# A decoder block on one core: attention halves stored apart and added by a loading DMA, first norms squared token by token, ten weight blocks kept in split form

## The chip, the core and the metric

The kernel runs on one core of one Trainium2 chip. The metric is device time in microseconds (us): the median of three runs of the kernel before is 1899.0 us (1898.85, 1899.0 and 1906.92). One further execution was taken by the hardware profiler; it took 1905.2 us, and its trace spans 1903.5 us. All durations and waits below come from that one execution.

The engines are named as in the profile: PE is TensorE (PEld its weight loads), DVE is VectorE, ACT is ScalarE, POOL is GpSimd, and SP is the queue that issues nearly all DMAs. Each engine, and the SP queue, works strictly in the order of its own instructions, and each instruction waits for the semaphores of what it needs.

## What is computed

One layer over 2048 tokens of width 1024, in float32:

```python
hn = rmsnorm(h, norm1_g)
proj = jnp.einsum('bsd,de->bse', hn, w_in)          # 1024 -> 2048: pool | q | k | v, 512 each
y_pool = pool_mixer(u_pool, pool_w, pool_scale)     # causal means over 2, 4, 8, 16 tokens
o = stick_breaking_attention(to_heads(q), to_heads(k), to_heads(v))   # 8 heads of 64
mixed = jnp.concatenate([rmsnorm(y_pool, pool_out_g), rmsnorm(y_attn, attn_out_g)], axis=-1)
h = h + jnp.einsum('bse,ed->bsd', mixed, w_out)
hn2 = rmsnorm(h, norm2_g)
act = jnp.square(jax.nn.relu(jnp.einsum('bsd,df->bsf', hn2, w_up)))
h = h + jnp.einsum('bsf,fd->bsd', act, w_down)
return rmsnorm(h, final_g)
```

## The kernel before

**Tiles.** The tokens are cut into NT = 4 tiles j of 512. Activations are held transposed: 128 features on the partitions, 512 tokens along the row. Every float32 operand of a product is *split* into a high and a low part in TensorE's own format (`split`, lines 142 to 146: ACT copies the high part at L145, DVE subtracts it at L146), and a product is three matmuls, high by high, high by low and low by high (L177 to L179).

**Input projection.** `w_in` is 16 blocks c of 1024 x 128; blocks 0 to 3 give the pool branch, 4 to 7 q, 8 to 11 k, 12 to 15 v. A block is loaded as one float32 tile `raw` of 512 KB (`load_raw`, two buffers) and split in two halves, *granules*, into tiles `hl` (`weights`, five buffers, WAHEAD = 5). A granule `hl` holds both parts and is again 512 KB. A product over one block is 24 matmuls into a PSUM tile `pd`, which has two buffers. `front(q)` treats the token tiles in pairs, (0, 1) and (2, 3). Six blocks (6, 10, 14, 7, 11, 15) are used for both tiles of a pair while they lie split in `hl`. The other ten, `EARLY` and `POOL`, are loaded and split anew for each of the four token tiles.

**First norm.** For tile 0 the squares are taken at once (`norm1_first`). For tiles 1 to 3 `norm1_rms` queues eight pieces of work: ACT squares a 128 x 512 chunk of the transposed x, DVE adds it to a sum `ss`. Then `mean_squares` sums over the partitions with matmuls by a column of 1/n (L204, PSUM tile `pm`), and `inv_root` computes the inverse root on POOL in small steps. `spread` (L230, tile `pr`) broadcasts it over the partitions with PE.

**Attention.** Weights of nearby keys alone are computed in the main path (`near`); a branch at the end handles the rest if any weight is left, and it isn't taken here. A unit is one head and two blocks of 128 queries: logits `pz` (L616, L617), two sigmoids on ACT (`sh`, `sg`), a mask on POOL (L647), a running product and a product on DVE, transposes `pta` (L663), a split into `at`, and products with v into `po` (L675). `po` holds the sum of the two parts in two halves of 64 partitions. `halves_sum` copies one half to SBUF on ACT (L633) and adds the other on DVE (L634), into a tile `ot` (one buffer) that two heads share; when both are in, one DMA of 256 KB stores it to `os_` in DRAM (L682). `attn_norm` later loads `os_` in two DMAs of 512 KB (L796, into `yb` for tiles 0 and 1, into `ol` for 2 and 3) and takes squares of what it loaded.

**What sets the order.** The Python code queues work in a list (`prog`) of products and notes, with small pieces (`later`) and attention units (`todo`) put between them by paces. Then a scheduler that models the times places every engine's instructions, the DMA issues among them. So the order on each engine is fixed before the run, and with a change in one place it moves everywhere in this first part. The first part (input projection, attention, output projection) fills the trace to about 690 us. After it come the up and down projections (PSUM tiles `pX`, `pY`, `pZ`, `pb`), done by a scheme with seven products in place of eight, which the change doesn't touch.

The DRAM tiles `hs` are read at the end by POOL's accumulating DMAs (L1249, `add_residual`), which load from DRAM and add to what stands in SBUF. They are the only ones of that kind before the change.

Of the kernel before, what the change touches and what calls it, by code (L numbers as in the profile page):

```python
# [15 lines left out]
P = 128  # L16
# [28 lines left out]
@with_exitstack  # L45
def hymba_block(ctx: ExitStack, tc: tile.TileContext, xT, gains, w_in, pool_w, w_out, w_up, w_down, out):
    nc = tc.nc
# [81 lines left out]
    vs = [[dram.tile([P, T], F32R, name=f"vs{h}_{j}") for j in range(NT)] for h in range(H)]  # L129
    os_ = [dram.tile([H // 2, P, T], F32, name=f"os{j}") for j in range(NT)]  # L130
# [25 lines left out]
    def load_raw(i):  # L156
        while len(raws) <= min(i, len(wlist) - 1):
            raw = wp.tile([P, 2, G, P], F32, tag="raw", name="raw")
            last_load[0] = nc.sync.dma_start(raw, wlist[len(raws)].rearrange("p (x k) c -> p x k c", x=2))
# [47 lines left out]

    def inv_root(pm, eng):
# [3 lines left out]
        nc.vector.tensor_scalar(m, pm, 1.0, EPS, op0=ALU.mult, op1=ALU.add)  # L212
        eng.tensor_scalar(y.bitcast(I32), m.bitcast(I32), -0.5, float(0x5F3759DF), op0=ALU.mult, op1=ALU.add)
# [19 lines left out]

    def inv_rms(ss, n, r=None, eng=None, early=False):

        eng = eng or nc.gpsimd
        with tc.high_priority():
            y = inv_root(mean_squares([ss], n, psz if early else None, "pz" if early else "px"), eng)
            yr = tmp.tile([P, 2, TB], F32R, tag="yr", name="yr")
            eng.tensor_copy(yr[:, 0], y)  # L240
            eng.tensor_tensor(yr[:, 1], y, yr[:, 0].bitcast(F32), ALU.subtract)
            where, tag = (psx, "px") if eng is nc.vector else (psz, "pz") if early else (pst, "pt")
            pr = where.tile([P, T], F32, tag=tag, name="pr")
            marks["pr"] = spread(pr, yr)
            if eng is not nc.vector:
                g = state["tick"]
                gates.extend([(g + 10, marks["pm"]), (g + 14, marks["pr"])])
# [38 lines left out]

    wlist = []
    prog = []

# [17 lines left out]
    def start():  # L307
# [4 lines left out]
        def weight(c, x):  # L312
            nc.sync.dma_start(raws[c][:, x], wlist[c][:, x * G:(x + 1) * G])

# [32 lines left out]

    def norm1_rms(j):
        def square(k):
            if k == 0:  # L350
                st[j]["ss"] = sum_tile()
            add_square(st[j]["ss"], st[j]["x"][:, k], k == 0)
        later.extend(lambda k=k: square(k) for k in range(KD))
        later.append(lambda: st[j].update(r=inv_rms(st[j]["ss"], D, root_tile() if j == 2 else None, early=j == 1)))

# [92 lines left out]
    def in_proj(j, c, again=False):  # L448
        if not again:
            wlist.append(w_in[c])  # L450
        if c < 4:
# [103 lines left out]
    def tail(first):  # L555
# [24 lines left out]
        for j in range(NT):  # L580
# [3 lines left out]
            for c in range(KD):  # L584
# [10 lines left out]
                if c == 3 and j == NT - 1:  # L595
                    note(begin_ffn)
                wlist.append(w_out[c])
                step(2, lambda w, j=j, c=c: dense(j, "m", w, lambda ps: add_acc(j, c, ps)))
# [37 lines left out]
    def near_unit(j, h, p, t):  # L636
# [40 lines left out]
        if p == 1:  # L677
            if h % 2 == 0:
                t["ot"] = ots[j, h // 2] = att.tile([P, T], F32, tag="ot", name="ot", bufs=1)
# [5 lines left out]
    ots, stages = {}, []  # L685

# [51 lines left out]
    def far(j):  # L738
        first = 2 if j == 0 else 0
        for h in range(H):  # L740
# [38 lines left out]
            on = att.tile([P, T], F32, tag="sh", name="onear")  # L779
            nc.sync.dma_start(on[me, f0:], os_[j][h // 2][me, f0:])  # L780
            nc.vector.tensor_tensor(ot[me, f0:], ot[me, f0:], on[me, f0:], ALU.add)
            nc.sync.dma_start(os_[j][h // 2][me, f0:], ot[me, f0:])


    def attn_norm(j, make=None):
        part = {}

        def load():
# [854 lines left out]
```

## Time and profile before

| | |
|---|---|
| median of three runs | 1899.0 us |
| the profiled execution: time / span of its trace | 1905.2 / 1903.5 us |
| DVE busy | 1480.9 us (78%) |
| ACT busy | 1023.7 us (54%) |
| POOL busy | 242.1 us (13%) |
| DMA packets | 535.91 MB, mean 282 GB/s |

A row of the page's groups reads: line, engine, operation, out<-in and shapes, number, then busy time and the mean of one in ns, then how long the engine stood idle just before them and what ended that. A row of waits reads: who waited, for whom, total us, times, longest. A row of the table by stages reads: the stage, its length, busy us of each engine with the number of instructions, the granted clock of TensorE, the share of the DMA engines' time, and GB/s.

Work beside PE in the first part is spread over DVE, ACT and the DMA queue as follows:

```profile
50.00:100.00 50.00, 49.30 (x242) 41.07 (x241) 43.60 (x79) 27.41 (x48) 16.43 (x35) 1.00 0.65 212
```

Here DVE is busy for 43.60 of 50 us, ACT for 27.41, and PE for 49.30.

### The profile page before, as it was taken

How to read it: one execution, taken by the hardware profiler on the slowest of the kernel's cores; microseconds unless marked ns; L12 is line 12 of the kernel's file. 1: busy time of each engine (PE TensorE's matmuls, PEld its weight loads, DVE VectorE, ACT ScalarE, POOL GpSimd, SP SyncE). 2: the span in 40 equal slices, each digit the busy share in tenths (PEclk: the TensorE clock that was granted, in tenths of full speed). 3: DMA queues.
4: the chain of work that ended last, by engine and by line, in shares of the span. 5: the costliest groups of instructions: out<-in, count | busy, mean ns of one | idle time of the engine just before them, and what ended most of it. 6: DMA issues, size and time to landing. Idle time of an engine off the chain costs nothing.

```text
span 1903.5 us, 26682 instructions
## 1 busy us (share of the span) xinstructions
PE 1869.5 (98%) x8883; PEld 1555.5 (82%) x8883; DVE 1480.9 (78%) x2151; ACT 1023.7 (54%) x1616; POOL 242.1 (13%) x463
## 2 busy tenths in 40 slices
PE   9999999999999999999999999999999999999997
PEld 7888788888888888778888888887788888888886
DVE  6887799668866976778699988786566677888774
ACT  5565466555544465554557555554332665656543
POOL 0333233223421050000000000000010010020120
PEclk9999999999999999999999999999999999999998
DMA  6686696798788867887899888889999899999752
GB/s 224 204 269 196 191 308 213 239 322 278 272 316 306 296 229 254 284 306 276 286 365 334 313 300 278 301 284 326 378 311 326 289 322 301 334 297 342 290 210 91
DMA packets 222164, 535.91 MB, mean 282 GB/s; under 512 B 26048, under 2 KB 32192, under 8 KB 218176
## 3 DMA queue, kind: packets, MB, share of 16 engines
q1 hardware_dynamic: 217264, 525.46, 79.2%
q0 software_dynamic: 4608, 8.39, 2.4%
q8 instruction: 72, 1.18, 0.3%
q14 instruction: 76, 0.62, 0.1%
q10 hardware_dynamic: 144, 0.26, 0.0%
HBM read 349.46 MB, written 184.55 MB: 281 GB/s over the span
## 4 chain that ended last, share of the span: by engine, by line
PE 45%; DMA 6%; DVE 4%; issue 2%; ACT 1%; POOL 0%; SPq 0%; DVEq 0%; ACTq 0%
PE pb L1274 14%; PE pb L1451 12%; PE pY L1101 10%; PE pZ L1101 5%; PE pX L1101 2%; DMA ar<-sd 1%; DVE hw L146 1%; DMA ar<-sdi 1%; PE pb L1391 1%; DMA t<-in_w_down_dram 1%; DMA su<-hs 0%; DMA sd<-a 0%; DMA td<-t 0%; DMA sdi<-a 0%; DMA b<-in_w_down_dram 0%
## 5 line engine op out<-in xcount | busy, mean ns | idle before, releaser
L1101 PE MATMUL pY<-sa,hw 128*128 128x512 f32 x1536 | 366.3, 389 | 3.0 <-ACT u L1024 2.6
L1101 PEld LDWEIGHTS pY<-sa,hw 128*128 128x128 f32 x1536 | 288.0, 188 | 64.3 <-ACT u L1024 3.9
L1274 PE MATMUL pb<-ad,wd 128*128 128x512 f32 x1344 | 305.1, 389 | 0.3 <-DVE ad L146 0.3
L177 PE MATMUL pd<-h,hl 128*128 128x512 f32 x752 | 299.0, 398 | 3.5 <-DVE acc L813 2.0
L179 PE MATMUL pd<-h,hl 128*128 128x512 f32 x752 | 297.6, 396 | 0.0
L178 PE MATMUL pd<-h,hl 128*128 128x512 f32 x752 | 297.5, 396 | 0.0
L1274 PEld LDWEIGHTS pb<-ad,wd 128*128 128x128 f32 x1344 | 252.2, 188 | 53.1 <-DVE ad L146 0.7
L1451 PE MATMUL pb<-ad,wd 128*128 128x512 f32 x1104 | 253.9, 390 | 2.4 <-ACT ad L145 2.0
L1451 PEld LDWEIGHTS pb<-ad,wd 128*128 128x128 f32 x1104 | 206.5, 188 | 46.1 <-ACT ad L145 2.4
L146 DVE TENSOR_TENSOR ad<-ar,ad 128x1024 fp32r<-128x1024 f32 x160 | 193.9, 1220 | 44.6 <-ACT ad L145 44.2
L145 ACT ACTIVATE ad<-ar 128x1024 fp32r<-128x1024 f32 x160 | 168.2, 1053 | 95.2 <-PE pb L1451 32.0
L1101 PE MATMUL pZ<-sa,hw 128*128 128x512 f32 x768 | 187.0, 390 | 1.1 <-DVE a L1044 1.0
L1101 PEld LDWEIGHTS pZ<-sa,hw 128*128 128x128 f32 x768 | 143.7, 188 | 32.4 <-DVE a L1044 2.6
L177 PEld LDWEIGHTS pd<-h,hl 128*128 128x128 f32 x752 | 142.6, 190 | 31.8 <-issue 2.8
L145 ACT ACTIVATE hl<-raw 128x512 fp32r<-128x512 f32 x168 | 104.2, 631 | 116.2 <-PE pd L179 66.1
L179 PEld LDWEIGHTS pd<-h,hl 128*128 128x128 f32 x752 | 142.5, 189 | 28.2
L178 PEld LDWEIGHTS pd<-h,hl 128*128 128x128 f32 x752 | 142.5, 190 | 26.8
L146 DVE TENSOR_TENSOR hl<-raw,hl 128x512 fp32r<-128x512 f32 x168 | 113.9, 684 | 45.8 <-ACT hl L145 45.5
L1018 ACT ACTIVATE a<-a 128x512 f32<-128x512 f32 x96 | 60.1, 629 | 97.4 <-DVE a L1060 43.0
L146 DVE TENSOR_TENSOR hw<-rt,hw 128x512 fp32r<-128x512 f32 x128 | 86.3, 683 | 26.0 <-ACT hw L145 26.0
L145 ACT ACTIVATE wd<-wq 128x1024 fp32r<-128x1024 f32 x56 | 59.3, 1060 | 76.8 <-PE pb L1274 68.1
L146 DVE TENSOR_TENSOR wd<-wq,wd 128x1024 fp32r<-128x1024 f32 x56 | 68.4, 1221 | 34.2 <-ACT wd L145 34.2
(218 smaller groups left out, 2736.2 us busy)
## 6 DMA issues: line engine op xcount, KB each, us to landing
ar<-sd SPq DMA_DIRECT2D x96, 512.0 KB, 5.7
ar<-sdi SPq DMA_DIRECT2D x64, 512.0 KB, 5.8
rb<-in_w_up_dram SPq DMA_DIRECT2D x30, 1024.0 KB, 6.6
sd<-a SPq DMA_DIRECT2D x104, 256.0 KB, 5.1
raw<-in_w_in_dram SPq DMA_DIRECT2D x50, 512.0 KB, 4.8
sdi<-hr SPq DMA_DIRECT2D x96, 256.0 KB, 5.5
wr<-in_w_down_dram SPq DMA_DIRECT2D x48, 512.0 KB, 5.6
sd<-s SPq DMA_DIRECT2D x88, 256.0 KB, 4.7
```

The lines of the kernel that those rows point to most:

```text
L145: nc.scalar.activation(hi, src, AF.Copy)
L146: return nc.vector.tensor_tensor(lo, src, hi.bitcast(F32), ALU.subtract)
L177: nc.tensor.matmul(ps, hl[:, 0, c], hi, start=(k == 0), stop=False)
L178: nc.tensor.matmul(ps, hl[:, 0, c], lo, start=False, stop=False)
L179: mm = nc.tensor.matmul(ps, hl[:, 1, c], hi, start=False, stop=(k == n - 1))
L1018: nc.scalar.activation(t, src, AF.Relu)
L1101: nc.tensor.matmul(t, w[:, wx, c], a[:, ax, c % 2], start=first and c == 0 and x == 0, stop=last and c == G - 1 and x == 2, skip_group_che ...
L1274: nc.tensor.matmul(b, t[:, wx, 2 * (kk % 2) + c, i * P:(i + 1) * P], a[:, ax, c], start=p in ("P1", "P5", "P2") and kk == 0 and c == 0 and ...
L1391: nc.tensor.matmul(b[:, cols], block(t, wx, c, n), a[:, ax, c, cols], start=False, stop=(i == 1 and c == 1 and x == 2), skip_group_check=True)
L1451: nc.tensor.matmul(ps[q, n], block(t, wx, c, n), left_[q][:, ax, c], start=(n_ in ("P1", "P3") and kk == 0 and c == 0 and x == 0), stop=(n ...
```

## The change

Three edits.

1. **Ten blocks kept split.** The first time that a block of `EARLY + POOL` is split, each `hl` is also stored to a DRAM tile `ws` (20 stores of 512 KB). The three later uses load `hl` straight from there, 512 KB for each granule, in place of a 512 KB load for two granules and two splits. So 60 of 168 splits go from ACT and from DVE, 30 loads of `raw` go, and 60 loads of `hl` come.
2. **First norms by tokens.** For tiles 1 to 3 a second copy of x with tokens on the partitions is loaded in eight tiles `xrow` of 256 KB. ACT squares each with its accumulator output, which leaves the sum of each token's 512 squares in one column of `ss`. POOL adds two columns for each token. The seven adds of DVE and the matmuls of `mean_squares` go for these three norms.
3. **Halves stored apart.** ACT copies the whole of `po` (128 x 512) to `ot`, and two DMAs of 128 KB for each head store its halves to `os_[j][0]` and `os_[j][1]`; the add on DVE goes. `attn_norm` loads the first halves with SP as before and then adds the second ones with two accumulating DMAs of 512 KB that POOL issues. A wait is added by that: POOL's DMA waits for the SP load into the same tile.

```diff
+    ws = {c: [dram.tile([P, 2, G, P], F32R, name=f"ws{c}_{x}") for x in range(2)] for c in EARLY + POOL}
...
     def load_raw(i):
         while len(raws) <= min(i, len(wlist) - 1):
+            if wlist[len(raws)][1] == "split":
+                raws.append(None)
+                continue
...
-            last_split[0] = split((hl[:, 0], hl[:, 1]), raws[i // 2][:, i % 2])
+            use, kept = wlist[i // 2][1:]
+            if use == "split":
+                nc.sync.dma_start(hl.bitcast(F32), kept[i % 2].bitcast(F32))
+            else:
+                last_split[0] = split((hl[:, 0], hl[:, 1]), raws[i // 2][:, i % 2])
             grans.append(hl)
             load_raw(i // 2 + 1)
+            if use == "keep":
+                nc.sync.dma_start(kept[i % 2].bitcast(F32), hl.bitcast(F32))
...
     def norm1_rms(j):
+        def load(k):
+            nonlocal rows
+            rows = ntp.tile([P, T], F32, tag="nt", name="xrow")
+            nc.sync.dma_start(rows, x[j, k // 2, :, k % 2])
...
-            add_square(st[j]["ss"], st[j]["x"][:, k], k == 0)
+                parts = sum_tile()
+            nc.scalar.activation(rows, rows, AF.Square, accum_out=parts[:, k:k + 1])
+            if k + 1 < KD:
+                load(k + 1)
+        def total():
+            two = parts[:, 0:KD].rearrange("p (b i) -> p b i", i=2)
+            nc.gpsimd.tensor_tensor(parts[:, KD:KD + TB], two[:, :, 0], two[:, :, 1], ALU.add)
...
-            halves_sum(ots[j, h // 2], po, h % 2)
-            if h % 2:
-                nc.sync.dma_start(os_[j][h // 2], ots.pop((j, h // 2)))
+            ot = att.tile([P, T], F32, tag="ot", name="ot", bufs=1)
+            nc.scalar.activation(ot, po, AF.Copy)
+            me = slice(h % 2 * DH, (h % 2 + 1) * DH)
+            for x in range(2):
+                nc.sync.dma_start(os_[j][x, h // 2, me], ot[x * DH:(x + 1) * DH])
...
-                nc.sync.dma_start(ol[i], os_[j][2 * i:2 * i + 2].rearrange("c p t -> p c t"))
+                nc.sync.dma_start(ol[i], os_[j][0, 2 * i:2 * i + 2].rearrange("c p t -> p c t"))
+            for i in range(2):
+                nc.gpsimd.dma_start(ol[i], os_[j][1, 2 * i:2 * i + 2].rearrange("c p t -> p c t"), accum_op=ALU.add)
```

How it moves instructions, at three places. The line numbers are each kernel's own; in the changed one L146 and L147 split, L173 loads a kept granule, L679 is the mask and L828 and L830 are the two loads of the attention's halves.

**ACT, up to the attention norm of tile 0** (second pair of tiles, near 360 us in the trace): the rows from the second `mix` tile, whose store stands just ahead of SP's load of `yb`, to the first square `ss` of that load. Before:

```order
343 L145 ACTIVATE mix<-nt 128x512
344 L437 ACTIVATE vf<-pd 128x512
345 L145 ACTIVATE mix<-nt 128x512
346 L145 ACTIVATE hl<-raw 128x512
347 L145 ACTIVATE vt<-ptv 128x8x64
348 L145 ACTIVATE mix<-nt 128x512
349 L437 ACTIVATE vf<-pd 128x512
350 L145 ACTIVATE hl<-raw 128x512
351 L184 ACTIVATE ss<-yb 128x512
```

And in the changed kernel, where the second `mix` stands in row 302:

```order
306 L146 ACTIVATE mix<-nt 128x512
307 L467 ACTIVATE vf<-pd 128x512
308 L146 ACTIVATE hl<-raw 128x512
309 L146 ACTIVATE vt<-ptv 128x8x64
310 L146 ACTIVATE at<-pta 128x512
311 L654 ACTIVATE sh<-pz 128x512
312 L656 ACTIVATE sg<-pz 128x512
313 L146 ACTIVATE qk<-pd 128x512
314 L654 ACTIVATE sh<-pz 128x512
315 L656 ACTIVATE sg<-pz 128x512
316 L146 ACTIVATE hl<-raw 128x512
317 L194 ACTIVATE ss<-yb 128x512
```

Seven rows stand between the second `mix` and the square before, and fourteen in the changed kernel (303 to 316): the first square of the loaded halves has moved back by seven instructions.

**POOL, at the same norm**: in the changed kernel the two accumulating loads stand between an inverse root and the masks of the next attention units; before there was nothing there.

```order
188 L253 CAST yr<-v 128x4
189 L254 TENSOR_TENSOR yr<-v,yr 128x4
190 L830 DMA yb<-os_244 128x2x512 x2
191 L679 AFFINE_SELECT sg<-sg 128x2x128
192 L691 COPY left_139<-pc 128x2
193 L679 AFFINE_SELECT sg<-sg 128x2x128
```

Whatever these loads wait for, the masks behind them now wait for too.

**SP, at the attention norm of tile 1** (near 410 us): `h<-mx` loads operands of the output projection, `mx` is where the normed branches are stored, `vs` holds v. Before:

```order
336 L547 DMA h<-mx_4_252 128x1024
337 L547 DMA h<-mx_5_253 128x1024
338 L547 DMA h<-mx_6_254 128x1024
339 L796 DMA yb<-os_245 128x2x512 x2
340 L609 DMA qa<-qs_2_174 128x512
341 L701 DMA vw<-vs_2_234 128x128
342 L703 DMA vw<-vs_3_235 128x512
343 L547 DMA h<-mx_7_255 128x1024
```

And in the changed kernel:

```order
422 L579 DMA h<-mx_4_252 128x1024
423 L579 DMA h<-mx_5_253 128x1024
424 L579 DMA h<-mx_6_254 128x1024
425 L828 DMA yb<-os_245 128x2x512
426 L474 DMA vs_2_238<-vt 128x512
427 L474 DMA vs_2_242<-vt 128x512
428 L173 DMA hl<-ws_1_287 128x1024
429 L579 DMA h<-mx_7_255 128x1024
430 L828 DMA yb<-os_245 128x2x512
431 L733 DMA vw<-vs_1_237 128x128
432 L714 DMA os_247<-ot 64x512 x2
433 L173 DMA hl<-ws_0_288 128x1024
```

Loads of kept granules, which PE needs within its next few products, now stand in one queue behind the burst of `h<-mx`.

More of the change, by code (lines that the diff above doesn't have):

```diff
@@ L45, in hymba_block @@
 @with_exitstack
-def hymba_block(ctx: ExitStack, tc: tile.TileContext, xT, gains, w_in, pool_w, w_out, w_up, w_down, out):
+def hymba_block(ctx: ExitStack, tc: tile.TileContext, xT, x, gains, w_in, pool_w, w_out, w_up, w_down, out):
     nc = tc.nc
@@ L246, in inv_rms @@
                 g = state["tick"]
-                gates.extend([(g + 10, marks["pm"]), (g + 14, marks["pr"])])
+                gates.extend(([(g + 10, marks["pm"])] if sums is None else []) + [(g + 14, marks["pr"])])
             if r is None:
@@ L287, in hymba_block @@
     wlist = []
+    used = set()
     prog = []
@@ L348, in norm1_rms @@
     def norm1_rms(j):
+        parts = rows = None
+        def load(k):
+            nonlocal rows
+            rows = ntp.tile([P, T], F32, tag="nt", name="xrow")
+            nc.sync.dma_start(rows, x[j, k // 2, :, k % 2])
         def square(k):
+            nonlocal parts
             if k == 0:
-                st[j]["ss"] = sum_tile()
-            add_square(st[j]["ss"], st[j]["x"][:, k], k == 0)
+                parts = sum_tile()
[5 more added lines that the diff above has]
+            nc.gpsimd.tensor_tensor(parts[:, KD:KD + TB], two[:, :, 0], two[:, :, 1], ALU.add)
+            st[j].update(r=inv_rms(None, D, root_tile() if j == 2 else None, early=j == 1, sums=parts[:, KD:KD + TB]))
+        later.append(lambda: load(0))
         later.extend(lambda k=k: square(k) for k in range(KD))
-        later.append(lambda: st[j].update(r=inv_rms(st[j]["ss"], D, root_tile() if j == 2 else None, early=j == 1)))
+        later.append(total)
     def norm1(j):
@@ L449, in in_proj @@
         if not again:
-            wlist.append(w_in[c])
+            use = "raw" if c not in ws else "split" if c in used else "keep"
+            used.add(c)
+            wlist.append((w_in[c], use, ws.get(c)))
         if c < 4:
@@ L596, in tail @@
                     note(begin_ffn)
-                wlist.append(w_out[c])
+                wlist.append((w_out[c], "raw", None))
                 step(2, lambda w, j=j, c=c: dense(j, "m", w, lambda ps: add_acc(j, c, ps)))
```

26 lines of the change are left out of this document (14 added, 12 removed).

## The prediction

> **What bounds the kernel now.** First the page's head and busy times:
>
> ```profile
> span 1903.5 us, 26682 instructions
> PE 1869.5 (98%) x8883; PEld 1555.5 (82%) x8883; DVE 1480.9 (78%) x2151; ACT 1023.7 (54%) x1616; POOL 242.1 (13%) x463
> ```
>
> PE is busy for 98%, but the end of a matmul is modelled, so I look for what ideal PE work looks like and then for what the first part has beyond it. From the table by stages, a stretch of the up projection and the two stretches of the first part with less than the full clock:
>
> ```profile
> 900.00:1000.00 100.00, 100.00 (x443) 82.62 (x441) 81.38 (x131) 56.44 (x98) 0.00 (x0) 1.00 0.90 323
> 200.00:250.00 50.00, 46.70 (x238) 39.18 (x237) 35.45 (x56) 26.77 (x50) 10.47 (x25) 0.93 0.76 238
> 450.00:500.00 50.00, 48.03 (x253) 40.72 (x252) 43.70 (x63) 31.73 (x58) 23.10 (x34) 0.93 0.83 277
> ```
>
> 443 matmuls of 512 columns in 100 us are 0.226 us each, with no gap: the later part can't gain. In the first part the clock is below 1 in two stretches; 7% of 50 us is 3.5 us lost in each. Then PE's waits between 60 and 600 us, where the edited code runs (engine, line, whom it waited for, us, times, longest):
>
> ```profile
> PE pp L396 <- ACT pls L145: 2.9, 3, 2.1
> PE pd L177 <- DVE acc L813: 1.8, 1, 1.8
> PE pr L230 <- POOL yr L240: 1.7, 1, 1.7
> PE pp L397 <- DVE pls L146: 1.4, 2, 1.2
> PE ptv L440 <- ACT vf L437: 1.3, 1, 1.3
> PE pd L177 <- DVE qk L146: 0.8, 1, 0.8
> PE pd L177 <- DVE qkr L423: 0.7, 1, 0.7
> PE po L675 <- DVE at L146: 0.7, 1, 0.7
> PE pr L230 <- POOL yr L241: 0.3, 1, 0.3
> PE ptv L440 <- DVE vf L435: 0.3, 1, 0.3
> ```
>
> They sum to 11.9 us, and all are for ACT, DVE or POOL being late. None is for a DMA. The timeline shows that the two slow stretches of the clock follow the longest of them:
>
> ```profile
> 206.58 0.51 PE L396 MATMUL pp<-pls,pw 128*128 128x512 f32 x1 [2.11 <-ACT pls L145]
> 208.27 0.80 PE L397 MATMUL pp<-pls,pw 128*128 128x512 f32 x1 [1.19 <-DVE pls L146]
> 456.20 0.33 PE L230 MATMUL pr<-identr,yr 128*128 128x128 f32 x1 [1.68 <-POOL yr L240]
> 456.82 0.91 PE L230 MATMUL pr<-identr,yr 128*128 128x128 f32 x3 [0.29 <-POOL yr L241]
> ```
>
> So all that this change can win is 11.9 us of waits, the two spells, and PE work that it removes. The profiled execution took 1905.2 us, 1.7 beyond its span and 6.2 above the median of 1899.0. Two spells are 7.0 us. I take it that the runs at 1898.85 and 1899.0 had no spell, and that the one at 1906.92 had them; no row shows this.
>
> **What goes.** Groups of the first part:
>
> ```profile
> L146 DVE TENSOR_TENSOR hl<-raw,hl 128x512 fp32r<-128x512 f32 x168 | 113.9, 684 | 45.8 <-ACT hl L145 45.5
> L145 ACT ACTIVATE hl<-raw 128x512 fp32r<-128x512 f32 x168 | 104.2, 631 | 116.2 <-PE pd L179 66.1 <-DMA raw<-in_w_out_dram 32.3 <-DMA raw<-in_w_in_dram 17.1
> L188 DVE TENSOR_TENSOR ss<-ss,sq 128x512 f32<-128x512 f32 x73 | 50.2, 687 | 5.5 <-ACT sq L187 4.6
> L634 DVE TENSOR_TENSOR ot<-ot,po 64x512 f32<-64x512 f32 x32 | 21.8, 681 | 9.7 <-ACT ot L633 9.3
> L633 ACT ACTIVATE ot<-po 64x512 f32<-64x512 f32 x32 | 19.0, 593 | 19.5 <-PE po L675 13.7 <-DMA os<-ot 5.4
> L437 ACT ACTIVATE vf<-pd 128x512 f32<-128x512 f32 x12 | 7.2, 600 | 12.0 <-PE pd L179 11.8
> L204 PE MATMUL pm<-inv,ss 128*128 128x1 f32 x120 | 14.3, 240 | 0.0
> L187 ACT ACTIVATE sq<-xt 128x512 f32<-128x512 f32 x28 | 17.0, 628 | 2.5 <-DVE ss L188 1.2 <-DVE mix L146 0.6 <-ACT sq L187 0.4
> ```
>
> - DVE loses 60 splits of 0.684 us (41.0), 21 adds of squares of 0.687 (14.4) and 32 adds of halves of 0.681 (21.8): 77 us.
> - ACT loses 60 copies of 0.631: 38 us. Copying 128 partitions of `po` in place of 64 costs it nothing (0.593 us against 0.600 for `vf`). No row has a square with the accumulator output; between nothing and a second pass of 0.63 it costs 24 x 0 to 0.63 = 0 to 15 us of ACT, spread over 300 us in which ACT is half idle. I take nothing.
> - PE loses three of the 15 sums by matmul: 14.3 / 15 = 0.95 us each, **2.9 us**. This is the one sure term, since PE has no cover.
>
> The 77 and 38 us lie beside PE and count only by the waits that they make shorter. How much a queue is clogged by splits shows in the waits of ACT and of SP:
>
> ```profile
> ACT hl L145 <- PE pd L179: 57.2, 42, 3.4
> SPq L159 <- DVE hl L146: 128.3, 46, 8.4
> ```
>
> ACT stands 57 us in a split that waits for PE to free a granule's buffer, with whatever is behind it (`pls`, `vf`) late. For 60 of 168 splits this wait moves to SP, as the wait of an `hl` load. But the scheduler has also planned PE's order anew for the lighter engines, so it spends part of the slack that it sees. Between 0 and 11.9 us I take half of the waits: **6.0 us**, since eight of the ten rows name DVE or ACT, whose rows splits are mixed into.
>
> **What comes.** DMA rows, and the busiest stretches of the stage table:
>
> ```profile
> raw<-in_w_in_dram SPq DMA_DIRECT2D x50, 512.0 KB, 4.8
> h<-mx SPq DMA_DIRECT2D x24, 512.0 KB, 8.5
> os<-ot SPq DMA_DIRECT2D x16, 256.0 KB, 5.2
> yb<-os SPq DMA_DIRECT2D x4, 512.0 KB, 8.6
> 0.00:50.00 50.00, 46.69 (x202) 35.67 (x203) 34.70 (x85) 29.37 (x50) 2.36 (x12) 1.00 0.70 223
> 400.00:450.00 50.00, 50.00 (x293) 43.15 (x292) 34.35 (x51) 27.04 (x50) 9.42 (x18) 1.00 0.99 344
> 550.00:600.00 50.00, 48.21 (x229) 40.15 (x228) 36.77 (x60) 25.43 (x44) 7.79 (x30) 1.00 0.99 382
> ```
>
> - Traffic: 30 `raw` loads go (15 MB), 60 `hl` loads (30), 20 stores (10) and 24 `xrow` loads (6) come, `os` is written and read twice as much (8): 39 MB more on 535.91. A kept granule must land within the time of the four other buffers, 4 x 12 x 0.226 = 10.9 us at least. Loads of 512 KB take 4.8 to 8.5 us, so they are hidden unless the queue is backed up. I take nothing here; the bad end is the second rival.
> - Early: in the first 100 us ACT and SP gain squares, `xrow` loads and 20 stores. The stores wait for splits that SP's next `raw` load waits for anyway. With 12 MB on some 22 (212 and 223 GB/s, from the row below and the stage row shown with the profile) the queue stays under the 382 GB/s that it showed. Between 0 and 3 us (one late granule) I take **1.0 us**.
> - `os` stores: each `ot` must have landed before the next head's copy; 32 heads in the 540 us above are 17 us apart, against 5.2. Nothing.
> - The accumulating loads. Rows of the one place that has them, and ACT's timeline around the load of tile 0's halves:
>
> ```profile
> L1249 POOL DMA_DIRECT2D p<-hs x8: 856/888/1151, 1392.6 to 1401.6; - x8
> DMA to landing us min/median/max: 6.4/9.3/14.2
> 358.46 0.62 ACT L145 ACTIVATE mix<-nt 128x512 fp32r<-128x512 f32 x1
> 368.63 0.63 ACT L184 ACTIVATE ss<-yb 128x512 f32<-128x512 f32 x1 [0.87 <-DMA yb<-os]
> ```
>
> Before, the square of `yb` came 10.2 us after the second `mix`, with seven ACT rows between, and it still waited 0.87. Now the plain load must land (in about 11 us), then two accumulating loads in 6.4 to 14.2: 17 to 25 us. Fourteen rows stand between, 9.3 / 7 x 14 = 18.6 us at the old rate. ACT stands there for 0 to 7 us, and behind it are `at`, `qk` and the sigmoids that PE needs; POOL holds the masks behind its wait in the same way. PE can run on for one PSUM buffer of 24 matmuls, 5.4 us, less what was already used. At tiles 0 and 1 I take 1.5 us each, **3.0 us**; tiles 2 and 3 are loaded in the output projection, where the split granules are far enough ahead.
>
> The Trainium skill, *DMA: Bandwidth & Descriptors*, section "Anatomy of one DMA — SWDGE (gpsimd) path", fits a DMA issued from GpSimd as 2.0 us plus bytes over 436 GB/s, 3.2 us for 512 KB as an estimate. By that the 3.0 us would go and the time be 1891; the trace's 6.4 to 14.2 us for half the bytes speak against it for accumulating loads.
>
> **The sum.** Against the profiled execution: 1905.2 − 2.9 − 6.0 + 1.0 + 3.0 = 1900.3 with both spells, 1893.3 without. From the median, with no spell in it: 1899.0 − 4.9 = **1894.1**. I forecast 1894.
>
> **Rivals.**
> 1. *Slower: ACT and POOL stand behind the accumulating loads.* Where ACT stands longer than the 5.4 us that one PSUM buffer covers, PE stops. At 7 us with POOL's masks late on top, I price a place at 8 us of PE and a spell of 3.5; two places are 23 us, and 1899.0 − 2.9 − 6.0 + 23 = 1913. For: 9.3 us median for 256 KB. Against: the row order gives ACT seven more rows of time.
> 2. *The DMA queue is full.* Between 400 and 450 us its share is 0.99 at 344 GB/s, 17.2 MB. Nine granules (an estimate: 18 at 2.7 us each if PE did nothing else, and attention takes about half) add 2.4 MB, the second halves 1.0 and their stores 0.5: 21.1 MB at 382 GB/s is 55 us, so granules run 5 us late, and a spell: 1894.1 + 8.5 = 1903.
> 3. *The new order gives it back.* The waits come from planned against real times, and a new plan has as many: 1899.0 − 2.9 + 1 to 4 = 1897 to 1900, near the median of now.
> 4. *All waits go*: 1899.0 − 2.9 − 11.9 = 1884.
>
> **Chances.** What a measurement of this kernel can tell from no change is about 0.5%, 9.5 us: 1889.5 to 1908.5. Forecast (1889 to 1897) 0.42, of it 0.04 just below the bound; rival 3 0.20; rival 4 0.16, by its half-way stops under 1889.5 too; rival 2 0.10; rival 1 0.12, and 0.03 of rival 2 ends above. Faster 0.20, same 0.65, slower 0.15. The range leaves out the outer part of rival 4 and half of rival 1: 1885 to 1911.
>
> **What would show it.** Right: the sum of PE's waits for ACT and DVE before 600 us is near 6, ACT's waits for PE in splits fall by a third, three `pm` groups are gone. Rival 1 shows as ACT waits for `yb` of over 5 us and PE waits just after them, near 370 and 420 us. Rival 2 shows as PE waiting for DMA `hl`, with a DMA share of 1. Rival 3 shows as PE waits of the old size on other lines. I'd be wrong most simply if a spell follows any new wait of over 2 us in most runs.

## The result and the profile after

The changed kernel takes 1957.24 us (median of four runs, 1953.91 to 1961.37). Of the four runs of the kernel before that stand beside it three took 1898.85 to 1906.92 us and one 3806.74 us, twice as long, so its median with all four is 1902.96 us and without that one 1899.0. The recorded ratio is 1.0273, 95% interval [1.0245, 1.0302]. By it the changed kernel is 52 us slower (it puts the kernel before at 1905.2 us); by the two medians it is 54 or 58. The forecast was 1894 us, in a range of 1885 to 1911.

The page's head and busy times of the changed kernel:

```profile
span 1953.3 us, 26701 instructions
PE 1878.2 (96%) x8859; PEld 1560.4 (80%) x8859; DVE 1415.8 (72%) x2038; ACT 989.4 (51%) x1580; POOL 237.8 (12%) x474
DMA packets 237813, 576.82 MB, mean 295 GB/s; under 512 B 28128, under 2 KB 34272, under 8 KB 233824
```

All the work that was to go has gone: DVE runs 113 instructions fewer, and the rows of the three groups lose 78 us (77 were forecast; its busy time, which counts overlapping instructions once, falls by 65). ACT is 34 us lighter, and PE issues 24 matmuls fewer. The bytes came within 2 MB of the count (41 MB more than 535.91; 39 were forecast). Yet the span grew by 49.8 us, so PE must stand or run slowly for that long. PE's waits between 60 and 600 us (columns as before):

```profile
PE pd L187 <- DMA hl<-ws: 7.3, 4, 4.3
PE pz L648 <- issue: 6.4, 1, 6.4
PE pz L648 <- DMA kw<-ks: 5.0, 3, 3.2
PE po L707 <- DVE at L147: 2.2, 2, 2.1
```

Before, all ten rows named ACT, DVE or POOL. Now the three largest come from the DMA queue: two name a load, and "issue" at 293.4 us ended when the second `kw` load of a head landed. Two more waits lie just outside that window. One row of PE's timeline each (start, us, engine, line, operation, number, the idle time before it and its releaser):

```profile
35.97 0.80 PE L187 MATMUL pd<-h,hl 128*128 128x512 f32 x1 [3.19 <-ACT hl L146]
602.49 1.87 PE L214 MATMUL pm<-inv,ss 128*128 128x1 f32 x8 [19.30 <-DVE ss L198]
```

The second one, 19.3 us, is the largest in the program: the sum of squares of tile 2's attention branch, in the output projection. And the table by stages, its first two rows and that place:

```profile
0.00:50.00 50.00, 43.51 (x169) 32.67 (x170) 27.12 (x71) 24.31 (x45) 1.99 (x11) 0.90 0.94 339
50.00:100.00 50.00, 44.63 (x206) 35.66 (x205) 41.87 (x73) 28.37 (x52) 22.11 (x28) 1.00 0.99 339
583.00:598.00 15.00, 0.20 (x1) 0.00 (x0) 0.69 (x1) 0.00 (x0) 2.31 (x2) 0.68 1.07 335
598.00:606.00 8.00, 3.51 (x12) 3.20 (x13) 5.99 (x10) 6.77 (x12) 1.11 (x2) 0.50 1.03 417
```

In the first 100 us the DMA engines are full (0.94 and 0.99, at 339 GB/s; before 0.70 and 0.65, at 223 and 212). From 583 to 598 us PE, ACT and DVE all but stand still with the DMA engines full, and when PE resumes its granted clock is 0.50. ACT, POOL and SP at that place:

```profile
575.38 1.58 SPq L828 DMA_DIRECT2D ol<-os  x2
582.80 2.50 POOL L830 DMA_DIRECT2D ol<-os  x2 [18.15 <-DMA ol<-os]
583.65 0.33 SPq L163 DMA_DIRECT2D raw<-in_w_out_dram  x1
598.45 0.63 ACT L146 ACTIVATE hl<-raw 128x512 fp32r<-128x512 f32 x1 [16.32 <-DMA raw<-in_w_out_dram]
598.99 0.61 ACT L194 ACTIVATE ss<-ol 128x512 f32<-128x512 f32 x1
```

SP loads the first halves at 575, POOL's loads follow when those have landed, and a `raw` load is issued between the two. It lands 14.7 us later, at 598.35; the accumulating loads land 10.0 and 13.8 us after their issue, at 592.76 and 597.78. ACT waits 16.3 us for `raw`, the first square stands right behind that split, and PE's `pm` waits for the squares. Without that split the squares would hardly have come sooner, since the second accumulating load landed only 0.6 us before `raw`.

Where the time went overall can be counted without trusting single waits. For each matmul I take the time to the start of the next one, less what such a matmul usually needs (the 20th percentile of its form, at most 0.227 us), and sum that by stretch:

```
PE's time beyond ideal work, us
stretch, us   before  after
0-100            8.0   20.3
100-275         21.8   14.4
275-400         13.0   22.1
400-550         16.5   28.9
550-700          3.1   29.1
700-end         17.9   16.0
sum             80.3  130.8
```

The sums differ by 50.5 us, as the spans do. The untouched stretch behind 700 us differs by 1.9 with no cause, and by 4.9 in one run below, so differences under about 5 us aren't read. A gain shows between 100 and 275 us: both old waits at 206 and 208 us and their spell (the stretch at half the clock behind them) are gone. Three losses outweigh it: 12 us at the start, 21 us between 275 and 550, 26 us at tile 2's norm.

### The profile page after: what moved, and what is told of

The parts are those of the page before. It is cut to its first block, busy times and chain, and to the rows that moved or that the text cites. A ratio compares the mean times of both kernels' runs of the same rounds, so it can differ in the third digit from the quotient of the medians.

```text
span 1953.3 us, 26701 instructions
## 1 busy us (share of the span) xinstructions
PE 1878.2 (96%) x8859; PEld 1560.4 (80%) x8859; DVE 1415.8 (72%) x2038; ACT 989.4 (51%) x1580; POOL 237.8 (12%) x474
## 4 chain that ended last, share of the span: by engine, by line
PE 46%; DMA 5%; DVE 4%; issue 1%; ACT 1%; POOL 0%; SPq 0%; DVEq 0%; ACTq 0%
PE pb L1308 14%; PE pY L1135 11%; PE pb L1485 11%; PE pZ L1135 6%; PE pX L1135 3%; DMA ar<-sd 1%; DMA ar<-sdi 1%; DMA sdi<-a 1%; DVE hw L147 1%; DMA hn<-hs 1%; DMA t<-in_w_down_dram 1%; PE pb L1425 1%; DMA su<-hs 0%; DMA td<-t 0%; DMA sd<-s 0%
## 5 line engine op out<-in xcount | busy, mean ns | idle before, releaser
L147 DVE TENSOR_TENSOR ad<-ar,ad 128x1024 fp32r<-128x1024 f32 x160 | 193.9, 1220 | 42.1 <-ACT ad L146 41.6
L146 ACT ACTIVATE ad<-ar 128x1024 fp32r<-128x1024 f32 x160 | 168.3, 1053 | 92.6 <-PE pb L1485 31.9
L187 PEld LDWEIGHTS pd<-h,hl 128*128 128x128 f32 x752 | 144.3, 192 | 44.7 <-ACT hl L146 6.6
L189 PEld LDWEIGHTS pd<-h,hl 128*128 128x128 f32 x752 | 143.8, 191 | 32.6 <-DVE hl L147 3.1
L188 PEld LDWEIGHTS pd<-h,hl 128*128 128x128 f32 x752 | 144.4, 192 | 27.4
L146 ACT ACTIVATE hl<-raw 128x512 fp32r<-128x512 f32 x108 | 66.2, 630 | 95.7 <-PE pd L189 47.0
L147 DVE TENSOR_TENSOR hw<-rt,hw 128x512 fp32r<-128x512 f32 x128 | 86.4, 684 | 25.3 <-ACT hw L146 25.3
L147 DVE TENSOR_TENSOR hl<-raw,hl 128x512 fp32r<-128x512 f32 x108 | 72.4, 682 | 44.3 <-ACT hl L146 44.3
L146 ACT ACTIVATE wd<-wq 128x1024 fp32r<-128x1024 f32 x56 | 59.4, 1061 | 78.4 <-PE pb L1308 69.7
L681 DVE TENSOR_TENSOR_SCAN pc<-sh,later_keys 128x512 f32<-128x512 f32 (+1 forms) x64 | 77.9, 1224 | 28.1 <-ACT sh L654 28.1
```

The costliest lines, as they stand in the source:

```text
L146: nc.scalar.activation(hi, src, AF.Copy)
L147: return nc.vector.tensor_tensor(lo, src, hi.bitcast(F32), ALU.subtract)
L187: nc.tensor.matmul(ps, hl[:, 0, c], hi, start=(k == 0), stop=False)
L188: nc.tensor.matmul(ps, hl[:, 0, c], lo, start=False, stop=False)
L189: mm = nc.tensor.matmul(ps, hl[:, 1, c], hi, start=False, stop=(k == n - 1))
L681: nc.vector.tensor_tensor_scan(pc[:, c0:T][:, ::-1], sh[:, c0:][:, ::-1], later_keys[:, c0:][:, ::-1], 1.0, op0=ALU.mult, op1=ALU.max)
```

## The experiments

Theory A says that the accumulating loads cost most of it (rival 1, in another place); B that the DMA traffic does; C that the new order has as many waits as the old one. In every run the order on each engine is planned anew, so a run changes the order along with its edit. One pair is free of this: the engines of `h_pload` and `e_halves` below run the same instructions in the same order. In the fences `...` marks lines or words left out. Each ratio is to runs of the kernel before on the same chip, whose medians were 1902.7 to 1904.3 us; the profiled execution of a kernel differs from its median by up to 8 us.

### One edit at a time

`e_keep` has the first edit alone, `e_rows` the second, `e_halves` the third.

```diff
e_keep
...
+            if use == "keep":
+                nc.sync.dma_start(kept[i % 2].bitcast(F32), hl.bitcast(F32))
e_rows
...
-            add_square(st[j]["ss"], st[j]["x"][:, k], k == 0)
+            nc.scalar.activation(rows, rows, AF.Square, accum_out=parts[:, k:k + 1])
e_halves
...
-            halves_sum(ots[j, h // 2], po, h % 2)
+            nc.scalar.activation(ot, po, AF.Copy)
...
+                nc.gpsimd.dma_start(ol[i], os_[j][1, 2 * i:2 * i + 2].rearrange("c p t -> p c t"), accum_op=ALU.add)
```

> The kernel before with the first edit alone (ten blocks stored split, kept granules loaded). Theory A (the accumulating loads cost most: the 19.3 us wait of pm near 583 us, and ACT and POOL standing at tiles 0 and 1): 5 to 15 us slower than before (1904 to 1914), with the new waits before 100 us and for hl near 290 and 440 us. Theory B (DMA traffic of the kept blocks costs most): 30 to 50 us slower (1929 to 1949).

> The kernel before with the second edit alone (first norms squared by tokens from a second copy of x). Both theories: within 5 us of before (1894 to 1904): 2.9 us less of PE, 6 MB more of loads.

> The kernel before with the third edit alone (halves stored apart, second halves added by accumulating loads). Theory A: 20 to 35 us slower (1919 to 1934), a PE wait of over 10 us for the sum of squares of an attention norm in the output projection. Theory B: under 10 us slower.

| | median us | ratio | interval |
|---|---|---|---|
| e_keep | 1911.46 | 1.0042 | [1.0025, 1.0060] |
| e_rows | 1899.70 | 0.9989 | [0.9972, 1.0006] |
| e_halves | 1939.07 | 1.0176 | [1.0148, 1.0203] |

The third edit alone costs 34 us and has the same wait for `pm` (19.5 us). The first costs 8. The second is no difference that can be told from none. This is what theory A expected (5 to 15 us for the first edit, 20 to 35 for the third), and not B. Together they make +40 by the ratios, where the whole change has +52: the edits don't add.

### What of the third edit costs

`h_noacc` leaves the accumulating loads out, so the second halves are stored and never added. `h_pload` keeps them as plain POOL loads, which overwrite the first halves, so the sum is not formed; every engine's order is the same as in `e_halves`. `h_acc01` has them for tiles 0 and 1 only (tiles 2 and 3 lack their second halves). `h_plain` loads the second halves by SP into a tile of their own and DVE adds them. `h_late` puts six empty pieces of work ahead of the squares of tiles 2 and 3, so that PE reaches `pm` 48 matmuls later.

```diff
h_noacc
-                nc.gpsimd.dma_start(ol[i], os_[j][1, ...], accum_op=ALU.add)
h_pload
-                nc.gpsimd.dma_start(ol[i], os_[j][1, ...], accum_op=ALU.add)
+                nc.gpsimd.dma_start(ol[i], os_[j][1, ...])
h_acc01
-            for i in range(2):
+            for i in range(0 if make else 2):
                 nc.gpsimd.dma_start(ol[i], os_[j][1, ...], accum_op=ALU.add)
h_plain
...
+                nc.sync.dma_start(o2, os_[j][1, ...])
+                nc.vector.tensor_tensor(ol[i], ol[i], o2, ALU.add)
h_late
+        if make:
+            later.extend([lambda: None] * 6)
         later.extend(lambda k=k: square(k) for k in range(4))
```

> The third edit alone, with the two accumulating loads of each attention norm left out (the second halves are stored and never added, so the attention's sums lack them). Theory A (the accumulating loads are the cost of the third edit): within 4 us of the kernel before, no wait of pm over 3 us in the output projection. Theory D (the doubled stores of the halves and the re-planned order are the cost): still over 15 us slower than before.

> The third edit alone, with the second halves loaded by SP into a tile of their own and added by DVE (same bytes, no accumulating DMA). Theory A: within 6 us of before. Theory E (the extra bytes in the burst of loads are the cost, however they are added): 15 us slower or more.

> The third edit alone, with six empty pieces of work ahead of the squares of tiles 2 and 3, so that the planned order puts pm of tile 2 behind 48 more matmuls (11 us) and ACT's first square behind three more splits; the DMAs are the same. Theory F (the plan takes the accumulating load for shorter than it is, and in-order engines stand for it): the 19.5 us wait shrinks to 9 or less and the time falls by 8 to 14 us from that of the third edit alone. Theory G (the loads themselves are late for everything because the accumulating loads fill the DMA engines): the wait stays over 15 us.

> The halves edit alone with the accumulating loads left only at tiles 0 and 1; for tiles 2 and 3 the second halves are not added. If tile 2's place in the output projection carries the cost: 1904 to 1912, and no wait of PE over 5 us. If each place costs alike: 1917 to 1922. My prediction's placing (all of the cost at tiles 0 and 1) would leave it at 1930 or more.

> The halves edit alone with the same POOL loads in the same place, order, bytes and waits, but without accumulation: the second halves overwrite the first ones in place of being added. Every engine's order is the same as with accumulation. If the accumulation is what makes these loads slow (10 and 14 us for 512 KB) and fills the DMA engines: landing falls to 5 to 8 us and the time to 1903 to 1915. If POOL's queue, the wait for the first load and the place in the order cost it: landing stays over 9 us, the pm wait stays at 15 us or more, time 1930 to 1940.

| | median us | ratio | interval |
|---|---|---|---|
| h_noacc | 1901.47 | 0.9987 | [0.9977, 0.9997] |
| h_acc01 | 1916.18 | 1.0067 | [1.0047, 1.0087] |
| h_plain | 1920.64 | 1.0084 | [1.0065, 1.0103] |
| h_pload | 1927.78 | 1.0129 | [1.0109, 1.0148] |
| h_late | 1934.82 | 1.0166 | [1.0146, 1.0185] |

Without the loads, and with the order planned without them, nothing is lost: they are the whole price of the edit, 0.0189 of the time or 36 us. By place, tiles 0 and 1 carry 0.0080 (15 us) and tiles 2 and 3 the other 0.0109 (21 us). Counted by stretch as above, `e_halves` loses 13 us more than `h_noacc` between 275 and 550 us and 27 between 550 and 700, so the split by place is good to some 6 us. `h_acc01` came out above what "tile 2 carries it" allowed and below "each alike", so both places count. At tile 0 ACT's timeline in `h_acc01` shows what rival 1 had described:

```profile
374.15 0.63 ACT L184 ACTIVATE ss<-yb 128x512 f32<-128x512 f32 x1 [7.83 <-DMA yb<-os]
374.69 0.62 ACT L187 ACTIVATE sq<-yb 128x512 f32<-128x512 f32 x1
377.97 1.15 ACT L187 ACTIVATE sq<-yb 128x512 f32<-128x512 f32 x2 [2.67 <-DMA yb<-os]
```

and PE's timeline in the same run the cost of it:

```profile
380.15 0.69 PE L675 MATMUL po<-at,vw 128*128 128x256 f32 x2 [3.36 <-ACT at L145]
```

ACT stands 7.8 and 2.7 us for `yb`, `at` is late by that, and PE waits.

`h_pload` and `e_halves` differ in nothing but the accumulation. The times of POOL's loads from issue to landing (queue, number, KB, median us), first in `e_halves`:

```profile
yb<-os POOLq DMA_DIRECT2D x4, 512.0 KB, 9.9
ol<-os POOLq DMA_DIRECT2D x4, 512.0 KB, 10.2
```

and in `h_pload`:

```profile
yb<-os POOLq DMA_DIRECT2D x4, 512.0 KB, 7.7
ol<-os POOLq DMA_DIRECT2D x4, 512.0 KB, 7.5
```

The table by stages, over the time in which they run at tile 2, for `e_halves`:

```profile
565.50:580.50 15.00, 0.68 (x3) 0.22 (x2) 0.69 (x1) 0.00 (x0) 2.25 (x2) 0.60 1.05 317
580.50:590.00 9.50, 4.28 (x14) 3.80 (x15) 6.66 (x11) 6.77 (x12) 1.80 (x3) 0.50 1.03 417
```

and for `h_pload`:

```profile
557.00:566.50 9.50, 0.44 (x2) 0.02 (x1) 0.69 (x1) 0.00 (x0) 1.33 (x2) 0.80 1.03 405
```

With the DMA engines equally full, 317 GB/s move while two loads accumulate and 405 while the same two only load. The queue of POOL's loads in these two stretches (packets, MB, share of the 16 engines), first in `e_halves`, then in `h_pload`:

```profile
q0 software_dynamic: 544, 1.05, 37.9%
q0 software_dynamic: 288, 1.05, 27.1%
```

The same bytes go in nearly twice as many packets when they accumulate. They take 37.9% of the 16 engines for 15.0 us, as much as all of them for 5.7 us, against 27.1% of 9.5 us, 2.6 us. So accumulation lengthens these loads by 2 to 3 us each and keeps the engines longer from what shares them. In the time it is 0.0047, 9 us, though the two intervals just touch. The other 27 us are there without any accumulation: in `h_pload` PE still waits 16.8 us for `pm`. Neither expectation held. The first (landings of 5 to 8 us, a time of 1903 to 1915) got the landings right; the second (landings over 9 us, a `pm` wait of 15 us or more, 1930 to 1940) got the wait right.

What those 27 us are, ACT's timeline at tile 2 shows. Before:

```profile
545.97 1.17 ACT L145 ACTIVATE hl<-raw 128x512 fp32r<-128x512 f32 x2
549.95 0.64 ACT L184 ACTIVATE ss<-ol 128x512 f32<-128x512 f32 x1 [2.81 <-DMA ol<-os]
...
564.56 1.16 ACT L145 ACTIVATE hl<-raw 128x512 fp32r<-128x512 f32 x2 [4.46 <-DMA raw<-in_w_out_dram]
```

and in `h_pload`:

```profile
570.24 0.63 ACT L145 ACTIVATE hl<-raw 128x512 fp32r<-128x512 f32 x1 [14.15 <-DMA raw<-in_w_out_dram]
570.77 0.61 ACT L184 ACTIVATE ss<-ol 128x512 f32<-128x512 f32 x1
```

Before, the squares waited for one load alone, and the split that waits for the slow `raw` stood behind them. Now the second load begins when the first has landed, so the squares moved back behind that split, and behind two bursts of 512 KB loads (`acc`, `raw`) that fill the engines. Both are late: the second of POOL's loads lands at 566.49 us in `h_pload` and `raw` at 570.13 (580.34 and 581.57 in `e_halves`), so the split adds 1 to 4 us to what the loads alone would cost the squares. In `h_plain`, where both halves load side by side, PE's wait for `pm` is 1.1 us, after as many matmuls as in `e_halves`: the serial pair with the order planned for it, not the bytes, made that wait. But that run still costs 16 us, with its waits on other lines (4.3 us for `qk` at tile 1, 4.3 for `hl` at 585): the twice as large read and DVE's adds have their own price, and I didn't part the two. `h_late` shrank the wait to 11.5 us, but its time is only 4 us below that of `e_halves` and the two intervals overlap: ACT still waited up to 16.6 us for `raw`. The wait lies between what its two expectations had named (9 or less, over 15). So "PE's row is planned too early" is at most a part of it; the loads are late in themselves.

### What of the first edit costs

`e_stores` keeps the 20 stores and goes on loading and splitting `raw`. `k_pool` lets POOL issue the stores. `k_second` stores a granule at its block's second use and loads it at the third and fourth only.

```diff
e_stores
-            use = "raw" if c not in ws else "split" if c in used else "keep"
+            use = "raw" if c not in ws else "raw" if c in used else "keep"
k_pool
-                nc.sync.dma_start(kept[i % 2].bitcast(F32), hl.bitcast(F32))
+                nc.gpsimd.dma_start(kept[i % 2].bitcast(F32), hl.bitcast(F32))
k_second
-            use = "raw" if c not in ws else "split" if c in used else "keep"
+            use = "raw" if c not in ws else ("raw", "keep", "split", "split")[used[c]]
```

> The kernel before with the 20 stores of split granules, but every later use still loaded raw and split (the stores are never read). It prices the stores alone: if the first 100 us are full because of them, 8 to 14 us slower (1907 to 1913) with the waits there; if the squares and xrow loads did it, within 3 us.

> The first edit alone, with its 20 stores issued by POOL instead of SP. If the stores cost by standing in SP's order (waiting for splits with raw loads behind them), the 8 us go: within 3 us of before. If they cost by their bytes in the first 100 us, the time stays 6 to 12 us over before.

> The kept granules alone, but stored at a block's second use (tile 1) and loaded at the third and fourth only: 20 stores and 40 loads, none of the stores in the first 100 us. If the price of this edit is the crowded first 100 us (24 MB where 20 were): 1897 to 1904, and no wait of PE over 1 us before 100 us that before does not have. If stores cost their bytes wherever they stand: 1908 to 1915.

| | median us | ratio | interval |
|---|---|---|---|
| e_stores | 1915.17 | 1.0069 | [1.0049, 1.0090] |
| k_pool | 1918.99 | 1.0073 | [1.0049, 1.0096] |
| k_second | 1912.01 | 1.0045 | [1.0031, 1.0059] |

The stores alone cost 13 us; the loads that follow seem to give some of it back (8 us for the whole edit), though the intervals overlap. Letting POOL issue them doesn't help: 14 us, above the 6 to 12 that the expectation had for a price of the bytes. Moving them out of the start doesn't either: `k_second` has 7.7 us beyond ideal work before 100 us, as before (8.0; `e_keep` 16.9), but loses as much elsewhere (3.8 us for an `hl<-ws` load at 422 us, 5.0 for `pm` at 555). "The crowded start" is the place of the loss in `e_keep`, not a price that can be dodged by moving the stores.

### What the edits cost together

`a_noacc` is the changed kernel without the accumulating loads (second halves not added). `c_kr` joins edits 1 and 2, `c_kh` 1 and 3, `c_rh` 2 and 3, the latter two without the accumulating loads (second halves not added). `c_k2r` is `c_kr` with the stores of `k_second`.

```diff
a_noacc, c_kh, c_rh
-                nc.gpsimd.dma_start(ol[i], os_[j][1, ...], accum_op=ALU.add)
c_k2r
-            use = "raw" if c not in ws else "split" if c in used else "keep"
+            use = "raw" if c not in ws else ("raw", "keep", "split", "split")[used[c]]
```

> All three edits without the two accumulating loads of each tile (the second halves are stored and not added). The single edits cost +8 (kept granules), -2 (norms by tokens), and -2 us (halves without the loads), +4 in all. If what the whole change costs beyond the sum of its parts (52 against 40 us) comes of the accumulating loads meeting the loads of kept granules: 1904 to 1910, no pm wait, no wait for hl<-ws over 1.5 us. If it comes of the kept granules standing behind the bursts of h<-mx in SP's queue, whatever POOL loads: 1914 to 1920, and the waits near 293 and 442 us stay.

> Kept granules and norms by tokens, without the halves edit. One by one +8 and -2 us. If their DMAs crowd each other in the first 100 us (10 MB of stores and 6 MB of xrow loads): 1918 to 1926, of it 12 us before 100 us. If the two add: 1906 to 1911. If the third edit is needed for the loss: the same 1906 to 1911.

> Kept granules and halves stored apart, without the accumulating loads (second halves not added). One by one +8 and -2 us. If the loads of kept granules and the doubled small stores of halves crowd SP's queue from 275 us on: 1918 to 1926, lost between 275 and 475 us. If they add: 1906 to 1911.

> Norms by tokens and halves stored apart, without the accumulating loads (second halves not added) and without kept granules. One by one -2 and -2 us. If kept granules are part of every loss: 1897 to 1904. If lighter ACT and DVE alone give a plan that comes too early: 1908 or more, with waits between 275 and 475 us.

> Kept granules and norms by tokens, as the run beside it, but the granules are stored at a block's second use and loaded at the third and fourth only. If the crowded first 100 us is where the pair loses: the loss before 100 us goes (12 us less than the run beside it). If the loads of kept granules between 275 and 475 us lose it: within 4 us of the run beside it.

| | median us | ratio | interval |
|---|---|---|---|
| a_noacc | 1929.58 | 1.0136 | [1.0117, 1.0155] |
| c_kr | 1927.58 | 1.0110 | [1.0084, 1.0136] |
| c_kh | 1915.24 | 1.0051 | [1.0029, 1.0072] |
| c_rh | 1908.19 | 1.0023 | [1.0009, 1.0037] |
| c_k2r | 1920.53 | 1.0075 | [1.0054, 1.0096] |

The sum of the parts without the loads was +4 us; `a_noacc` has +26. So more than the accumulating loads was missed, and both of my expectations for that run were too low. The pair of edits 1 and 2 makes nearly all of it: +21, where the two alone give +8 and -2. The other pairs lose less beyond their sums (`c_kh` +10 against +6, between its two expectations; `c_rh` +4 against -4, just at the bound of "lighter ACT and DVE alone"). PE's time beyond ideal work, counted as above:

```
stretch, us   before e_keep e_rows  c_kr c_k2r a_noacc
0-100            8.0   16.9   11.4  21.3   9.8   20.9
100-275         21.8   22.1   13.1  13.5  25.1   15.9
275-400         13.0    9.5   22.3  28.6  21.3   25.3
400-550         16.5   18.0   12.2  18.8  18.4   27.8
550-700          3.1    3.6    3.6   7.5   3.8    9.2
700-end         17.9   19.5   13.0  15.9  15.8   15.1
```

At the start the queue fills. The loads between 20 and 37 us, issue to landing (number, KB, median us), in the kernel before:

```profile
raw<-in_w_in_dram SPq DMA_DIRECT2D x4, 512.0 KB, 3.5
```

in `e_keep`, with stores but no `xrow` loads:

```profile
raw<-in_w_in_dram SPq DMA_DIRECT2D x2, 512.0 KB, 9.6
```

in `c_kr`:

```profile
ws<-hl SPq DMA_DIRECT2D x4, 512.0 KB, 8.8
xrow<-in_x_dram SPq DMA_DIRECT2D x4, 256.0 KB, 8.1
raw<-in_w_in_dram SPq DMA_DIRECT2D x2, 512.0 KB, 8.9
```

and in `c_k2r`:

```profile
xrow<-in_x_dram SPq DMA_DIRECT2D x8, 256.0 KB, 4.4
raw<-in_w_in_dram SPq DMA_DIRECT2D x4, 512.0 KB, 4.4
```

A weight block that took 3.5 us takes 9.6 beside the stores alone, 8.9 beside stores and `xrow` loads, and 4.4 beside the `xrow` loads without the stores. So the stores fill the queue here, and by the table the two edits' losses before 100 us only add up (8.9 and 3.4 us alone, 13.3 together). What the pair loses beyond the sum lies behind 275 us (some 18 us by the table). Without the early stores PE's early loss goes too (21.3 to 9.8), as expected. The time fell by only 7 us, and the intervals overlap: between 100 and 275 us 11.6 us come back, 9.4 of them in one wait for `qk` at 247 us. That a loss moves when the order is made anew is what theory C says.

Between 275 and 550 us two things are seen in the changed kernel's trace and were not tried apart. SP's timeline at 293 us, while PE waits 6.4 us for the second `kw` load:

```profile
291.01 2.40 SPq L458 DMA_DIRECT2D ks<-qk  x4
293.45 0.59 SPq L642 DMA_DIRECT2D qb<-qs  x1
294.14 1.27 SPq L714 DMA_DIRECT2D os<-ot  x2
295.46 0.60 SPq L643 DMA_DIRECT2D qb<-qs  x1
296.10 0.58 SPq L732 DMA_DIRECT2D kw<-ks  x1
296.73 0.49 SPq L734 DMA_DIRECT2D kw<-ks  x1
```

SP issues one DMA after the other, about 0.6 us each and with no gap; the load that PE needs stands last in such a run and lands only 2.9 us after its issue. Here it is the number of DMAs ahead of it rather than their bytes. At 443 us it looks like the bytes: `hl`, issued at 436.59 behind five loads of `h`, one of `yb` and two stores of `vs`, lands 10.6 us later, and PE waits 4.3 us. How the 22 us of the pair divide between such places and the new order stays open.

Of all these only `h_noacc` has an interval wholly below 1 (up to 0.9997), and it leaves the second halves out of the sum. `e_rows` (0.9989, up to 1.0006) is the only complete one that isn't slower.

## Why the prediction was wrong

- **The accumulating loads** were priced at 3.0 us, all of it at tiles 0 and 1. They cost 36 us in the edit alone and 26 (1.0273 against 1.0136) in the whole change. The step that failed is "tiles 2 and 3 are loaded in the output projection, where the split granules are far enough ahead". That was read off PE's small waits there before, without asking what stands behind the squares and the splits: `raw` took up to 10.6 us there already, and PE needs `pm` in its row whatever granules are ready. 21 us were there. The term for tiles 0 and 1 was 1.5 us each; it is 15 us together.
- **Rival 1** had the mechanism and its price per place was nearer (8 us, and 7.5 was measured at tiles 0 and 1). It counted two places of four, at a chance of 0.12. The duration behind it was right: 6.4 to 14.2 us was the bound taken from the 256 KB loads, 9.4 to 10.3 the medians measured for 512 KB. By the fit of the Trainium skill, *DMA: Bandwidth & Descriptors*, section "Anatomy of one DMA — SWDGE (gpsimd) path", 512 KB take 3.2 us, an estimate; the trace disagrees, with 7.5 us for the plain POOL load and 10.2 for the accumulating one, both beside other traffic.
- **Traffic** was taken at nothing: "the queue stays under the 382 GB/s that it showed". The bytes were right (34 MB in 100 us, and 339 GB/s was measured), the capacity was not: in the first 100 us the engines are full (0.94 and 0.99) at 339. The 382 came from a stretch of mostly loads; what makes the rate lower here, with 10 MB of stores of `ws` among the 34, no run tried apart (between 20 and 37 us `c_kr`, with such stores, moved 394). The early term of 1.0 us measured 12.3, and the first edit, costed at nothing net, costs 8 alone and 21 with the second. Rival 2 had the full queue, but at 400 to 450 us and for 8.5 us in all; the changed kernel waits 4.3 us for `hl` at 443 us and 3.2 for `kw` at 457.
- **Waits** were to fall by half of 11.9 us. Those of before did go (206, 208 and 456 us), but between 60 and 600 us others for ACT, DVE and POOL sum to 9.9 us, and 18.7 us of waits for the DMA queue stand beside them. Each edit alone shows the same: in `e_keep` and `e_rows` the waits at 206 and 208 us are gone as well, and one as large stands elsewhere (3.7 us for `qk` at 260 us, 2.4 for `pls` at 333). So lighter engines hardly made PE's waits for them smaller. Rival 3 said so in kind; its 1 to 4 us were too small a price, because it counted waits of the old size.
- **The base.** That the median of 1899.0 us had no spell in it was an assumption. Beside the experiments the kernel before had medians of 1902.7 to 1904.3 us, so the forecast also started some 4 to 5 us too low.
- **PE's matmuls**: 2.9 us of `pm` matmuls go (17.1 to 14.2 us in `e_rows`). That term was right. ACT's accumulator output costs 0.19 us a square, 4.5 us in all and on no path; taking nothing was right.

## What to carry to other kernels

Where PE is busy for 98%, taking work off engines that are not the bound can win only the waits that these engines cause; price the DMAs that are added in exchange first, stretch by stretch, against the rate that full engines reach there (339 and 382 GB/s in two stretches here), and by their number on the issuing queue too. A load that must wait for another load into the same tile at least doubles the latency of whatever reads it (at tile 2 from 8.0 us for the first loads to 16.5 for both in `h_pload`, and 22 with accumulation in `e_halves`), and where the order is fixed ahead, all that stands behind the reader stops as well. Edits that each cost little can cost more together (here +8 and -2 us alone, +21 as a pair): try them in pairs before adding up.

## What was not expected of the hardware

- Two accumulating loads lowered what the full DMA engines moved: 317 GB/s against 405 with the same loads plain. The accumulating ones went in 544 packets in place of 288 and held the engines about twice as long; a `raw` load of 512 KB beside them took 15.3 us in `e_halves` and 12.2 in `h_pload`.
- After the long stall the granted clock was 0.50 for some 6 us (from 602.5 us on), so the 19.3 us wait cost some 22 us of PE (half of 6 us more). Such stretches came with the waits of 3.2 (at 33 and at 457 us), 6.4, 4.3 and 19.3 us, and also with one of 2.1 us at 412 and one of 1.6 us at 650; six others of 1.0 to 1.8 us between 50 and 700 us had none. So the length of the last wait alone doesn't decide it.
- An SP queue with no gap between its DMAs issued one about every 0.6 us (ten in 6.2 us from 291.0 us on).
